# Seven block products for the first column pair of both retention output projections, with the last head's k-tiles late in the order

## The chip, the cores and the metric

The kernel runs on one core of a Trainium2 chip. The metric is the device time of one execution in microseconds (us). A core has TensorE (PE, matmuls), VectorE (DVE), ScalarE (ACT), GpSimd (POOL) and SyncE (SP); here the last two mostly start DMA transfers.

## The reference, cut to what matters

A trunk of two layers on 256 tokens with a model width of 2048: a gated linear attention layer, then a retention layer. Each normalises its input, projects it with `w_in`, mixes over the tokens in heads, gates the result with a SiLU and projects the 4096 inner columns back with `w_out`. The part around the change, in float32:

```python
o = from_chunks(o)                                   # retention: 8 heads x 512 columns
mu = jnp.mean(o, axis=-1, keepdims=True)
var = jnp.mean(jnp.square(o - mu), axis=-1, keepdims=True)
o = ((o - mu) * lax.rsqrt(var + EPS)).reshape(B, S, D_INNER).astype(h.dtype)
o = o * gn_g + gn_b
return (o * jax.nn.silu(gate)) @ w_out               # [256, 4096] @ [4096, 2048]
...
h = h + retention_mixer(...)
return rms_norm(h, final_norm)
```

## The kernel before

**Matmuls and weights.** The 256 tokens are two blocks of 128. Every fp32 product is made of three matmuls on values split into a high and a low part (`three`, `mm3`): hi by hi, hi by lo, lo by hi. Weights come from HBM in blocks of 512 KB, two k-tiles of 128 by 512 columns, on SyncE's queue. `emit_split` (L269) makes the two parts of a block: ScalarE copies the high part (L283), VectorE subtracts it to get the low one (L284). The splits are emitted up to three blocks ahead of use.

**Halves.** A layer's inner columns are worked in two halves. In the retention layer, half 0 is heads 0 to 3, half 1 heads 4 to 7. Behind the four heads of a half, `out_half` (L1022) multiplies their 16 k-tiles (4 per head, in `ogt`) by the `w_out` rows of the half and adds the result to the residual. The output's 2048 columns are four columns of 512, so two pairs, (0,1) and (2,3). The residual is read by `get_resid` (L458, 2 MB on GpSimd's queue). The last column of the last half is done by `out_tail`, which also makes the final norm.

**Plain and joint pairs.** A plain pair takes 192 matmuls of 128x512: 2 columns, 16 k-tiles, 2 token blocks, 3 parts. A joint pair (`out_pair`, L950) treats k-tiles 0 to 7 of two columns and two token blocks as a 2 by 2 block product and makes it of seven products (P1, P2, P3, P5, P6, P7, P8; 12 matmuls each), in the manner of Strassen; k-tiles 8 to 15 are taken directly, in steps v4 to v7 for the one column and g4 to g7 for the other (12 matmuls each). That is 180 matmuls. The products need sums of token blocks (`make_sums`, L420: VectorE sums, then split by ScalarE and VectorE) and sums of weight blocks. The latter are made in place: a DMA with accumulation onto a block that is in the core already (L292, on GpSimd's queue), or a sum of two blocks by VectorE (L278). A joint pair has 22 splits, a plain one 16. Results of products are added to or subtracted from the residual by VectorE (`join`, L962 and L964).

**What is joint.** `JOINT` says it for each layer and half. In the retention layer only the second pair of half 0 is joint. The first pair of each half is plain and comes in two parts: steps 0 to 5 of both columns (k-tiles 0 to 11), then the residual's load, then steps 6 and 7 of both (`CUT` = 6). The four k-tiles of the half's last head are 12 to 15, so they are wanted only in the second part.

**The last head's tail.** `ret_head` (L1239) computes queries and keys, values and gates of a head by a joint product of its own, in the order MIXED or, for heads 0 and 4, WHOLE. `ret_tasks` (L1153) is a head's mixing as a row of small tasks: rotary, scores, `ro_ps` (the head's output), group norm (`mv`, `rm`, `rh_nw`), scale and shift (L1207, L1219), the gate's product and the transposes to `ogt` (L679, L687). Each task is emitted at a step of later work: for the last head of a half, in the first column pair of the output projection, one task per step (`out_steps`). The token sums for half 0's second pair are a task as well.

**Order.** `_plan` writes out by hand the sequence of all weight blocks; `pair` (L72) that of a joint pair. A planner orders each engine's instructions from the emission, which `high_priority` can move ahead. An engine then works through its own list in order.

Of the kernel before, what the change touches and what calls it, by code (L numbers as in the profile page):

```python
# [10 lines left out]
F32 = mybir.dt.float32  # L11
# [44 lines left out]
def _plan():  # L56
# [38 lines left out]
                        post.append((x[j], (g, 2 + j)))  # L95
                    use(z[j] if tok in ("P3", "P7") else x[j], z[j] if tok == "P6" else None, post)

    def out_cols_of(name, half, cut, joint):
        for c in (0, 2):
            cols = [(name, half, c + n) for n in range(2)]  # L100
            if joint[c // 2]:
                pair(cols[1], cols[0])
                continue
            late = [range(NSUB)] if c or not cut else [range(cut), range(cut, NSUB)]
            for js in late:
                for x in cols:
                    plain(x, js)

    for half in range(2):
        for h in (2 * half, 2 * half + 1):  # L110
            plain(("aqk", h))
            for g in (2 * h, 2 * h + 1):
                if g in JOINT["a"]:
                    pair(("ag", g), ("av", g))
                else:
                    plain(("av", g))
                    plain(("ag", g))
        out_cols_of("ao", half, 0, JOINT["ao", half])
    for half in range(2):
        for h in range(4 * half, 4 * half + 4):  # L120
            pair(("rg", h), ("rv", h), ("rqk", h), ret_order(h))
        out_cols_of("ro", half, CUT, JOINT["ro", half])
    places = {k: n for n, k in enumerate(loads)}
    for _, _, post in subs:
        for _, k in post:
# [33 lines left out]


# [1 line left out]
def kernel(  # L162
# [106 lines left out]
    def emit_split(pieces=1, between=None):  # L269
        i = emitted["sub"]  # L270
        c, pre, post = subs[i]
        emit_raws(c)
        src = raws[c]
        for n in range(i + 1, min(i + 1 + EARLY, len(subs))):
            at, by = subs[n][:2]
            if by is not None and n not in added:
                added.add(n)
                nc.vector.tensor_tensor(raws[at], raws[at], raws[by], ALU.add)  # L278
        hi, lo = split_tiles(i)
        step = SUB // pieces  # L280
        for k in range(pieces):
            sl = slice(k * step, (k + 1) * step)
            a = nc.scalar.activation(hi[:, sl], src[:, sl], AF.Copy)  # L283
            b = nc.vector.tensor_tensor(lo[:, sl], src[:, sl], hi[:, sl].bitcast(F32), ALU.subtract)  # L284
            if i == 0:
                first(a, b)
                if k == 0:
                    between()
        splits[i] = (hi, lo)
        emitted["sub"] += 1  # L290
        for n, key in post:
            nc.gpsimd.dma_start(raws[n], block(key), accum_op=ALU.add)  # L292
        emit_raws(c)
# [126 lines left out]
    def make_sums(lhs, name, where):  # L420
        s = cur["s"] = [None] * 4
        room = where(name)
        tt = nc.vector.tensor_tensor
        y = [t4_p.tile([P, QK, SEQ], F32, tag="t4", name=f"{name}_y{i}") for i in range(2)]
        for i in range(2):
            part = lhs[:, i * QK : (i + 1) * QK].bitcast(F32)
            tt(y[i], part[:, :, 0, :], part[:, :, 1, :], ALU.add)
        yield
        one_, two = slice(0, P), slice(P, SEQ)
        f = [t4_p.tile([P, 2, QK, P], F32, tag="t4", name=f"{name}_f{i}") for i in range(2)]  # L430
        f3, f5, f6, f7 = f[0][:, 0], f[0][:, 1], f[1][:, 0], f[1][:, 1]
        tt(f5, y[0][:, :, two], y[1][:, :, two], ALU.subtract)
        tt(f6, f5, y[0][:, :, one_], ALU.subtract)
        yield
        tt(f3, f6, y[1][:, :, one_], ALU.add)
        tt(f7, y[0][:, :, one_], y[0][:, :, two], ALU.subtract)
        yield
        for i, x in ((0, f3), (1, f5), (2, f6), (3, f7)):
            if i % 2 == 0:
                two_ = room(i // 2)  # L440
                s[i], s[i + 1] = two_[:, 0], two_[:, 1]
            keep(nc.scalar.activation(s[i][:, :, 0, :], x, AF.Copy))
            keep(tt(s[i][:, :, 1, :], x, s[i][:, :, 0, :].bitcast(F32), ALU.subtract))
            if i % 2:
                yield
# [501 lines left out]
            f"xt2_{c}",  # L947
        )

    def out_pair(c, first, name):  # L950
# [8 lines left out]
        def join(col, t, src, op=ALU.add):  # L959
            dst = cur["resid"][:, t, col * GW : (col + 1) * GW]  # L960
            if op == ALU.add:
                keep(nc.vector.tensor_tensor(dst, src, dst, ALU.add))  # L962
            else:
                keep(nc.vector.tensor_tensor(dst, dst, src, ALU.subtract))  # L964

        def whole(col, t):
            if not first:
                square_sum(t, col)

        late = deque() if first else deque([out_transposes(c)])  # L970

        def turn():
            advance()
# [1 line left out]
                next(late[0], None)  # L975

        g = c + 1
        product(A, plain(0, 0), stop=True)
        advance()
        direct(lhs, (C, V1), 4)  # L980
        join(g, 0, A)
        advance()
        product(C, summed(0))
        advance()
        direct(lhs, (C, V1), 5)
        drain_side()
        product(P5, summed(1), stop=True)
        direct(lhs, (C, V1), 6)
        for t in range(2):
            join(c, t, P5)  # L990
        product(A, summed(2), stop=True)
        product(B, plain(4, 0))
        join(c, 0, A, ALU.subtract)
        direct(lhs, (C, V1), 7, stop=True)
        product(A, summed(3), stop=True)
        with tc.high_priority():
            keep(nc.scalar.activation(u3, A, AF.Copy))
        join(c, 0, C)
        whole(c, 0)
        direct(lhs, (B, A), 4)  # L1000
        join(c, 1, u3, ALU.subtract)
        join(c, 1, V1)
        whole(c, 1)
        direct(lhs, (B, A), 5)
        turn()
        product(A, plain(4, 1))
        turn()
        direct(lhs, (B, A), 6)
        turn()
        direct(lhs, (B, A), 7, stop=True)  # L1010
        join(g, 0, B)
        whole(g, 0)
        join(g, 1, A)
        whole(g, 1)
        if not first:
# [6 lines left out]
    def out_half(first, final, name, cut=0, hook=None, joint=(False, False)):  # L1022
        pend = {}
        for c in range(4):
            if joint[c // 2]:
                if c % 2 == 0:
                    out_pair(c, first, name)
                continue
            if final:
                fns[c] = gn_p.tile([P, GW], F32, tag="gn", name=f"fn{c}")  # L1030
                nc.gpsimd.dma_start(fns[c], final_norm[c * GW : (c + 1) * GW].partition_broadcast(P))
                if c == 3:
                    break
            if cut and c == 0:
                if True:
                    for i in range(2):
                        pend[i] = acc(2, f"{name}{i}_ps")
                        steps_x(pend[i], ogt, range(cut), lambda j: hook(i, j))
                    get_resid(f"{name}_resid")
                    for i in range(2):  # L1040
                        steps_x(pend[i], ogt, range(cut, NSUB), lambda j: hook(1, j))
            ps = pend[c] if c in pend else group_x(ogt, f"{name}{c}", deadline=None if c else 5)
            for t in range(2):
                out_cols(c, ps[t], t, first, final)
            if first or final:
# [193 lines left out]
    def ret_head(h):  # L1239
        lhs = xhl  # L1240
        mixed = h % 4 != 0
        at = (2, 3, 0, 1) if h < 4 else (0, 1, 2, 3)
        q_ps = [acc(1, f"rqk{h}_ps{c}", (P, 2, SEQ), [at[c + 2]])[0] for c in range(2)]
        q_ps += [lev_p.tile([P, 2, SEQ], F32, tag="lev", name=f"rqk{h}_ps{c}") for c in (2, 3)]
        if not mixed:
# [127 lines left out]
        begun.clear()  # L1373
        closed.clear()

    def out_steps(i, j):
        step()

    for h in range(2):
        gla_head(h)  # L1380
    slots = deque((2, 3, 0, 1))
# [25 lines left out]
    out_tail()  # L1407


# [98 lines left out]
```

## Time and profile before

| | |
|---|---|
| three timed runs | median 1381.45 us, 1380.05 to 1381.87 |
| the profiled execution | 1379.47 us |
| its span, first to last instruction | 1377.6 us |
| mean granted TensorE clock | 0.998 |
| last head of half 0 (head 3) | 853.5 to 921.4 us |
| first pair of half 0 (plain) | 921.4 to 970.3 us |
| second pair of half 0 (joint) | 970.3 to 1011.5 us |
| last head of half 1 (head 7) | 1212.7 to 1279.9 us |
| first pair of half 1 (plain) | 1279.9 to about 1330 us |

The stretches are read from the first and last starts of the tiles `ra_ps`, `rae_ps`, `re_ps` and `rb_ps`. In the rows, PE is a matmul, PEld the load of its stationary operand; a group's line gives source line, engine, operation, output<-inputs, shape and count, then busy us, the mean ns of one, and the idle time ahead of them with what ended it. Tile names: `ra`, `rb` are the output projections of half 0 and 1, an `e` behind it a joint pair (`rae_ps`), `re_ps` a head's values and gates, `rsum` token sums. A timeline's row gives start, duration, engine, line, operation and, in brackets, the idle time before it.

### The profile page before, as it was taken

Reading aid. Unit: us, or ns where it says so; the run is one execution under the profiler, and the core shown is the slowest. Engines: PE = TensorE matmul, PEld = TensorE weight load, DVE = VectorE, ACT = ScalarE, POOL = GpSimd, SP = SyncE. Lnnn points to the kernel's source line nnn. Section 1 sums busy time; section 2 is a strip of 40 time slices with the busy share of each in tenths; the row PEclk is TensorE's granted clock in tenths of the full one; section 3 lists DMA queues with packets and bytes.
Section 4 is the critical chain, followed back from the end, with each engine's and each line's share of the span. In section 5 each row is a group of like instructions: output and inputs, shape, how many; then the busy total and the mean of one; then the engine's idle time right before and its main releaser. Section 6 shows DMA issues by size and latency. Waiting matters only on the chain.

```text
span 1377.6 us, 18438 instructions
## 1 busy us (share of the span) xinstructions
PE 1366.5 (99%) x6632; PEld 1148.5 (83%) x6632; DVE 1079.1 (78%) x1497; ACT 836.0 (61%) x1104; POOL 131.8 (10%) x188
## 2 busy tenths in 40 slices
PE   9999999999999999999999999999999999999997
PEld 7888888888888888888888888888888888888887
DVE  6686795987878896769888888886858897888673
ACT  6576656656567747656666566655546666666452
POOL 1003020110021021001011010100101101010000
PEclk9999999999999999999999999999999999999999
DMA  9765556689658657858897878896798797879661
GB/s 359 245 182 160 172 177 187 151 250 343 204 153 265 204 175 180 314 168 247 279 317 202 256 203 247 208 310 206 184 372 238 217 271 193 256 199 327 211 191 62
DMA packets 83931, 312.94 MB, mean 227 GB/s; under 512 B 9712, under 2 KB 10736, under 8 KB 82560
## 3 DMA queue, kind: packets, MB, share of 16 engines
q1 hardware_dynamic: 67344, 242.64, 50.9%
q0 software_dynamic: 15056, 61.74, 22.6%
q10 hardware_dynamic: 1440, 7.38, 1.4%
q8 instruction: 52, 0.85, 0.2%
q14 instruction: 39, 0.32, 0.1%
HBM read 301.24 MB, written 10.49 MB: 226 GB/s over the span
## 4 chain that ended last, share of the span: by engine, by line
PE 99%; DMA 0%; DVE 0%; ACT 0%; DVEq 0%; issue 0%; SPq 0%
PE rqk_ps L364 8%; PE re_ps L392 8%; PE re_ps L391 8%; PE re_ps L393 8%; PE rqk_ps L365 4%; PE gqk_ps L364 4%; PE gg_ps L322 3%; PE gv_ps L321 3%; PE gv_ps L322 3%; PE gv_ps L323 3%; PE gg_ps L323 3%; PE gg_ps L321 3%; PE ge_ps L392 2%; PE ge_ps L393 2%; PE ge_ps L391 2%; PE gae_ps L391 2%
## 5 line engine op out<-in xcount | busy, mean ns | idle before, releaser
L284 DVE TENSOR_TENSOR lo<-raw,hi 128x1024 fp32r<-128x1024 f32 (+1 forms) x557 | 675.2, 1222 | 225.7 <-ACT hi L283 218.9
L283 ACT ACTIVATE hi<-raw 128x1024 fp32r<-128x1024 f32 (+1 forms) x557 | 584.5, 1056 | 390.8 <-PE gg_ps L323 49.0
L364 PE MATMUL rqk_ps<-xhl,hi 128*128 128x512 f32 x480 | 162.8, 397 | 0.0
L392 PE MATMUL re_ps<-lo,xhl 128*128 128x512 f32 x352 | 137.3, 390 | 0.0
L393 PE MATMUL re_ps<-hi,xhl 128*128 128x512 f32 x352 | 137.1, 390 | 0.0
L391 PE MATMUL re_ps<-hi,xhl 128*128 128x512 f32 x352 | 132.7, 391 | 0.0
L292 POOL DMA_DIRECT2D raw<-in_w_all x84 | 72.7, 867 | 530.3 <-DVE lo L284 283.8
L365 PE MATMUL rqk_ps<-xhl,lo 128*128 128x256 f32 x480 | 122.3, 280 | 0.0
L364 PEld LDWEIGHTS rqk_ps<-xhl,hi 128*128 128x128 f32 x480 | 89.5, 188 | 17.9
L365 PEld LDWEIGHTS rqk_ps<-xhl,lo 128*128 128x128 f32 x480 | 87.5, 189 | 3.4
L393 PEld LDWEIGHTS re_ps<-hi,xhl 128*128 128x128 f32 x352 | 66.1, 188 | 13.6
L391 PEld LDWEIGHTS re_ps<-hi,xhl 128*128 128x128 f32 x352 | 66.1, 188 | 13.3
L392 PEld LDWEIGHTS re_ps<-lo,xhl 128*128 128x128 f32 x352 | 66.1, 188 | 13.1
L364 PE MATMUL gqk_ps<-xhl,hi 128*128 128x512 f32 x216 | 76.5, 398 | 0.0
L322 PE MATMUL gg_ps<-lo,xhl 128*128 128x512 f32 x192 | 75.4, 393 | 0.0
L322 PE MATMUL gv_ps<-lo,xhl 128*128 128x512 f32 x192 | 75.2, 392 | 0.0
L321 PE MATMUL gv_ps<-hi,xhl 128*128 128x512 f32 x192 | 75.1, 393 | 0.0
L323 PE MATMUL gv_ps<-hi,xhl 128*128 128x512 f32 x192 | 75.0, 391 | 0.0
L323 PE MATMUL gg_ps<-hi,xhl 128*128 128x512 f32 x192 | 74.9, 390 | 0.0
L321 PE MATMUL gg_ps<-hi,xhl 128*128 128x512 f32 x192 | 74.8, 391 | 0.0
L365 PE MATMUL gqk_ps<-xhl,lo 128*128 128x256 f32 x216 | 59.0, 280 | 0.0
L801 POOL TENSOR_TENSOR s<-s,m 128x64 f32<-128x64 f32 x56 | 36.1, 676 | 232.7 <-DVE m L792 223.4
(407 smaller groups left out, 2682.5 us busy)
## 6 DMA issues: line engine op xcount, KB each, us to landing
raw<-in_w_all SPq DMA_DIRECT2D x451, 512.0 KB, 4.8
raw<-in_w_all POOLq DMA_DIRECT2D x84, 512.0 KB, 6.5
resid<-in_x_n SPq DMA_DIRECT2D x2, 1024.0 KB, 9.1
gg<-in_gn_g POOLq DMA_DIRECT2D x8, 256.0 KB, 3.9
resid_x<-resid ACTq DMA_DIRECT2D x1, 2048.0 KB, 9.1
gb<-in_gn_b POOLq DMA_DIRECT2D x8, 256.0 KB, 6.2
gb_resid<-resid_x POOLq DMA_DIRECT2D x1, 2048.0 KB, 11.8
resid_g<-gb_resid ACTq DMA_DIRECT2D x1, 2048.0 KB, 8.9
```

Of the source, the lines that this page charges most:

```text
L283: a = nc.scalar.activation(hi[:, sl], src[:, sl], AF.Copy)
L284: b = nc.vector.tensor_tensor(lo[:, sl], src[:, sl], hi[:, sl].bitcast(F32), ALU.subtract)
L292: nc.gpsimd.dma_start(raws[n], block(key), accum_op=ALU.add)
L321: mm(ps, xh, hi[:, q, :], start=kt == 0, stop=False)
L322: mm(ps, xh, lo[:, q, :], start=False, stop=False)
L323: mm(ps, xl, hi[:, q, :], start=False, stop=kt == NKT - 1)
L364: mm(ps[c], wh, rhs[:, kt, :, :], start=kt == 0, stop=False)
L365: mm(ps[c][:, 0, :], wl, rhs[:, kt, 0, :], start=False, stop=False)
L391: mm(ps, xh, hi[:, q, :], start=start, stop=False, **again)
L392: mm(ps, xh, lo[:, q, :], start=False, stop=False, **again)
L393: mm(ps, xl, hi[:, q, :], start=False, stop=stop, **again)
L801: nc.gpsimd.tensor_tensor(dst, dst, side_of(m[:, li, :], z), ALU.add)
```

## The change

In both halves of the retention layer the first column pair becomes joint; half 0 then has two joint pairs, half 1 one, and its columns 2 and 3 stay as they were. `CUT`, the two-part steps and their hook go. The first pairs take a new order, LATE, in which P6 stands ahead of P2, v6 and v7 come later, and the last head's k-tiles (v6, v7, g6, g7) are used late. The token sums of both halves are made within the half's last head (`making`, at q3, q4, P5, q5 and g7), the second working tile of them in another pool; the residual is read at the last head's v7. In `out_pair` the first four steps emit a task of the last head each, a product's joins are emitted one step after it, and the squares and the final norm's product follow once all joins of a column and token block are out. The rows of the final norm are read at the start of the pair (`norm_row`). In `emit_split` a weight sum is emitted at the earliest with its own split, and not while its block must still be split plain.

```diff
-    def out_cols_of(name, half, cut, joint):
+    def out_cols_of(name, half, joint):
         for c in (0, 2):
             cols = [(name, half, c + n) for n in range(2)]
             if joint[c // 2]:
-                pair(cols[1], cols[0])
+                pair(cols[1], cols[0], order=out_order(name, c))
                 continue
...
+LATE = "P1 v4 z P3 v5 P5 P6 P2 v6 P7 g4 g5 v7 P8 g6 g7"
+
+
+def out_order(name, c):
+    return LATE if (name, c) == ("ro", 0) else UNIT
...
-CUT = 6
 EARLY = 2
 JOINT = {
     "a": (5, 7),
     ("ao", 0): (True, True),
     ("ao", 1): (False, True),
-    ("ro", 0): (False, True),
-    ("ro", 1): (False, False),
+    ("ro", 0): (True, True),
+    ("ro", 1): (True, False),
 }
...
-        for n in range(i + 1, min(i + 1 + EARLY, len(subs))):
+        for n in range(i, min(i + 1 + EARLY, len(subs))):
             at, by = subs[n][:2]
-            if by is not None and n not in added:
+            if by is not None and n not in added and all(subs[m][0] != at for m in range(i, n)):
                 added.add(n)
                 nc.vector.tensor_tensor(raws[at], raws[at], raws[by], ALU.add)
...
+        toks = [x for x in out_order(name[0] + "o", c).split() if x != "z"]
+        for n, tok in enumerate(toks):
+            if tok[0] == "P":
+                products[tok]()
+            else:
+                direct(lhs, (C, V1) if tok[0] == "v" else (B, A), int(tok[1:]), stop=tok[1:] == str(NSUB - 1))
+            if tok == "P7":
+                with tc.high_priority():
+                    keep(nc.scalar.activation(u3, A, AF.Copy))
+            while pend:
+                pend.pop(0)()
+            if tok in joins:
+                pend.append(joins[tok])
+            if n < 4:
+                advance()
+                step()
+                if n == 3:
+                    drain_side()
+            elif tok in ("g5", "P8", "g6"):
+                turn()
...
     def ret_head(h):
...
-        at = (2, 3, 0, 1) if h < 4 else (0, 1, 2, 3)
+        at = (2, 3, 0, 1)
...
+        last = h % 4 == 3
+        making = make_sums(ogt, f"rsum{h}", sums_in_v, "next_s", sg_p) if last else None
+
         def turn(tok):
             n = toks.index(tok)
+            if last and tok in ("q3", "q4", "P5", "q5"):
+                next(making)
+            if last and tok == "v7":
+                get_resid(f"resid{h}")
...
+                if last and tok == "g7":
+                    for _ in making:
+                        pass
...
     slots = deque((0, 1, 2, 3))
-    tasks.append(make_sums(ogt, "rsum", sums_in_v))
-    out_half(True, False, "ra", CUT, out_steps, JOINT["ro", 0])
+    cur["s"] = cur["next_s"]
+    out_half(True, False, "ra", JOINT["ro", 0])
...
-    slots = deque((2, 3, 0, 1))
-    out_half(False, True, "rb", CUT, out_steps)
+    slots = deque((0, 1, 2, 3))
+    cur["s"] = cur["next_s"]
+    out_half(False, True, "rb", JOINT["ro", 1])
```

More of the change, by code (lines that the diff above doesn't have):

```diff
@@ L101, in out_cols_of @@
             if joint[c // 2]:
-                pair(cols[1], cols[0])
+                pair(cols[1], cols[0], order=out_order(name, c))
                 continue
[L104 to L107, printed above, removed]
+            for x in cols:
+                plain(x)
     for half in range(2):
@@ L948, in out_transposes, with out_pair @@
         )
-    def out_pair(c, first, name):
+    def out_pair(c, first, final, name):
         lhs, s = ogt, cur["s"]
@@ L957, in out_pair, with whole, turn, join @@
         u3 = t4_p.tile([P, 2, GW], F32, tag="t4", name=f"{name}e{c}_u3")[:, 0, :]
-        def join(col, t, src, op=ALU.add):
+        if final:
+            for col in (c, c + 1):
+                norm_row(col)
+        def whole(col, t):
+            if not first:
+                square_sum(t, col)
+            if final:
+                dst = cur["resid"][:, t, col * GW : (col + 1) * GW]
+                nc.vector.tensor_tensor(dst, dst, fns[col], ALU.mult)
+        onward = not (first or final)
+        late = deque([out_transposes(c)] if onward else [])
+        def turn():
+            advance()
+            if late:
+                next(late[0], None)
+        g = c + 1
+        tt_done, pend = set(), []
+        def join(col, t, src, op=ALU.add, mark=None):
             dst = cur["resid"][:, t, col * GW : (col + 1) * GW]
@@ L964, in join @@
                 keep(nc.vector.tensor_tensor(dst, dst, src, ALU.subtract))
[L966 to L973, printed above, removed]
-            if late:
[L975 to L1015, printed above, removed]
+            tt_done.add((col, t, mark))
+            if all((col, t, m) in tt_done for m in parts[col - c][t]):
+                whole(col, t)
@@ new lines, in out_pair @@
+        parts = ((("5", "6", "v"), ("5", "7", "v")), (("1", "g"), ("g",)))
+        products = {
+            "P1": lambda: product(A, plain(0, 0), stop=True),
+            "P2": lambda: product(B, plain(4, 0)),
+            "P3": lambda: product(C, summed(0)),
+            "P5": lambda: product(P5, summed(1), stop=True),
+            "P6": lambda: product(A, summed(2), stop=True),
+            "P7": lambda: product(A, summed(3), stop=True),
+            "P8": lambda: product(A, plain(4, 1)),
+        }
@@ L1016, in out_pair @@
+        join(g, 0, B, mark="g")
+        join(g, 1, A, mark="g")
+        if onward:
             for _ in late[0]:
@@ L1026, in out_half @@
                 if c % 2 == 0:
-                    out_pair(c, first, name)
+                    out_pair(c, first, final, name)
                 continue
             if final:
-                fns[c] = gn_p.tile([P, GW], F32, tag="gn", name=f"fn{c}")
-                nc.gpsimd.dma_start(fns[c], final_norm[c * GW : (c + 1) * GW].partition_broadcast(P))
+                norm_row(c)
                 if c == 3:
                     break
[L1034 to L1042, printed above, removed]
+            ps = group_x(ogt, f"{name}{c}", deadline=None if c else 5)
             for t in range(2):
```

31 lines of the change are left out of this document (22 added, 9 removed).

## The prediction, made before the change was run

> **What bounds the kernel now.** I read the page's head and its chain of waits first, then windows around the two retention output projections, then single tiles and engines there. The page:
>
> ```profile
> span 1377.6 us, 18438 instructions
> ...
> PE 1366.5 (99%) x6632; PEld 1148.5 (83%) x6632; DVE 1079.1 (78%) x1497; ACT 836.0 (61%) x1104; POOL 131.8 (10%) x188
> ...
> PE 99%; DMA 0%; DVE 0%; ACT 0%; DVEq 0%; issue 0%; SPq 0%
> ```
>
> The last line is the chain that ended last: TensorE holds 99% of it, nothing else a whole per cent. So every matmul taken away is worth its spacing, as long as TensorE never has to wait. VectorE's 78% is a mean, and the windows (PE, PEld, DVE, ACT, POOL busy, then granted clock, DMA share, GB/s) show what it hides:
>
> ```profile
> 853.50:921.40 67.90, 67.90 (x339) 57.40 (x338) 59.16 (x80) 42.30 (x55) 7.44 (x10) 1.00 0.85 254
> 921.40:970.30 48.90, 48.90 (x221) 40.57 (x220) 34.64 (x51) 24.97 (x33) 2.86 (x4) 1.00 0.74 215
> 970.30:1011.50 41.20, 41.20 (x184) 34.12 (x183) 34.59 (x34) 23.97 (x23) 3.45 (x4) 1.00 0.85 264
> ...
> 1212.70:1279.90 67.20, 67.20 (x335) 56.89 (x334) 56.50 (x76) 42.46 (x55) 6.62 (x9) 1.00 0.85 259
> ```
>
> These are head 3, the first (plain) column pair of the first half, its second (joint) pair, and head 7. TensorE is busy in all of each. The plain pair leaves VectorE 14 us free, the joint pair 6.6 us, the heads 9 to 11.
>
> **The saving.** The change makes the first pair of each half joint: 180 matmuls of 128x512 for 192, so 24 fewer in all; the order of the built program has 24 fewer on TensorE too. A joint pair that is there now gives the price:
>
> ```profile
> L391 PE MATMUL rae_ps<-hi,ogt x44: 389/389/389, 970.4 to 1010.7; 128*128 128x512 f32 x44
> ...
> L393 PE MATMUL rae_ps<-hi,ogt x44: 389/389/389, 970.8 to 1011.2; 128*128 128x512 f32 x44
> ```
>
> 180 matmuls start from 970.4 to 1011.2: 40.8/179 = 0.228 us each, and 24 x 0.228 = **5.5 us saved**.
>
> **What the change adds on VectorE.** Per pair: 6 more hi and lo splits (22 for 16), two weight sums, four accumulate loads, some joins; and the last head's tail (group norm, gate, transposes), which the plain pair spread over its 192 matmuls, must now be done before the last head's k-tiles are wanted. Let T0 be the first matmul of the new pair. The built order before P7, the sixth product, is P1 v4 P3 v5 P5 P6 P2 v6: with one stray matmul 97, and 8 transposes. The transposes and VectorE's prices in the present heads and pairs:
>
> ```profile
> 945.88 0.82 PE L679 MATMUL rot_tp<-ident,ro 128*128 128x128 f32 x6
> ```
>
> ```profile
> L284 DVE TENSOR_TENSOR lo<-raw,hi 128x1024 fp32r<-128x1024 f32 x74 | 89.6, 1224 | 26.8 <-ACT hi L283 25.4
> L278 DVE TENSOR_TENSOR raw<-raw,raw 128x1024 f32<-128x1024 f32 x4 | 4.7, 1220 | 0.0
> L962 DVE TENSOR_TENSOR ra_resid<-rae_ps,ra_resid 128x512 f32<-128x512 f32 x5 | 3.4, 687 | 0.1
> ...
> L443 DVE TENSOR_TENSOR rsum<-rsum_f,rsum 128x512 fp32r<-128x512 f32 x4 | 2.6, 684 | 0.0
> ...
> L427 DVE TENSOR_TENSOR rsum_y<-ogt 128x1024 f32<-128x1024 f32 x2 | 2.4, 1220 | 0.0
> ```
>
> The last numbers are means of one from start to end. Back to back they overlap, as VectorE's timeline of the present tail shows (start, duration):
>
> ```profile
> 919.95 3.50 DVE L284 TENSOR_TENSOR lo<-raw,hi 128x1024 fp32r<-128x1024 f32 x3
> ...
> 924.96 0.69 DVE L1326 TENSOR_TENSOR rsg<-re_ps,rsg 128x512 f32<-128x512 f32 x1
> ...
> 931.86 0.75 DVE L1207 SCALAR_TENSOR_TENSOR ro<-ro,mv,gg 128x512 f32<-128x512 f32 x1
> ...
> 932.72 0.17 DVE L471 TENSOR_SCALAR rh_nw<-rm 128x2 int32<-128x2 int32 x1
> 932.80 1.22 DVE L284 TENSOR_TENSOR lo<-raw,hi 128x1024 fp32r<-128x1024 f32 x1
> ...
> 934.13 0.16 DVE L474 SCALAR_TENSOR_TENSOR rh_nw<-rh_nw,rm 128x2 f32<-128x2 f32 x1
> 934.33 0.16 DVE L475 TENSOR_TENSOR rh_nw<-rh_nw 128x2 f32<-128x2 f32 x1
> ...
> 937.50 1.42 DVE L1219 SCALAR_TENSOR_TENSOR ro<-ro,ra,gb 128x512 f32<-128x512 f32 x2
> ...
> 939.96 1.29 DVE L1155 TENSOR_TENSOR ro<-ro,rsg 128x512 f32<-128x512 f32 x2
> ```
>
> Spacings: a lo (3.50-1.22)/2 = 1.14; a 128x512 sum 1.29-0.69 = 0.60; a scalar-tensor-tensor 1.42-0.75 = 0.67; a tiny 128x2 0.20 where it needs the one before, 0.08 where not. The weight sum has the lo's shape and duration, so 1.14.
>
> P7 writes the bank that holds P6's result until VectorE has subtracted it from the residual, and in VectorE's built list that join stands behind P7's own two lo halves. From the last head's gate join (L1326) to it the list holds, in either half, 13 lo (14.8), 2 weight sums (2.3), 10 sums of 128x512 (6.0), 2 scalar-tensor-tensor (1.3), 14 tiny, ten of them chained (2.3), and the join itself, 0.7: **27.4 us without a pause**. It starts about T0-0.3:
>
> ```profile
> 925.25 0.39 PE L322 MATMUL ra_ps<-lo,ogt 128*128 128x512 f32 x1
> ...
> 928.88 0.39 PE L671 MATMUL ro_ps<-rv,rsc 128*128 128x512 f32 x1
> ```
>
> The gate join waits for its bank: now it starts at 924.96, 0.29 before the first matmul behind the gate's, at 925.25. And what stands ahead of it, the L1207 pair, passes at 931.86+0.67 = 932.53, 3.65 behind the last ro_ps matmul at 928.88; in the new order that matmul is 17 matmuls, 3.9 us, before T0. So the join of P6 ends at about T0+27.1. TensorE's own work ahead of P7 is 97 x 0.228 = 22.1, and 8 transposes at some 0.1 (six from first start to last end take 0.82) make 22.9. **P7 comes 4.2 us late, in each half.** About half is lost at P6 already: its first lo half is 9.9 us of list ahead of the join's end, T0+17.2, where TensorE would want it at T0+15.1 (62 matmuls, 8 transposes). From P7 on there are 84 matmuls, 19 us, against 7 splits (8.0) and five joins (3.0) on VectorE: it catches up, and nothing else is late.
>
> ScalarE has less: its hi copies are 1.06 us, thirteen of them 13.8 of the 27.
>
> ```profile
> L283 ACT ACTIVATE hi<-raw 128x1024 fp32r<-128x1024 f32 x74 | 78.0, 1059 | 56.6 <-PE ra_ps L323 20.7 <-PE rae_ps L393 12.4 <-PE rqk_ps L364 7.7
> ```
>
> **The accumulate loads.** A weight sum is undone for the later product by loading the block once more, on GpSimd's queue. In the joint pair that is there:
>
> ```profile
> 981.36 0.86 POOL L292 DMA_DIRECT2D raw<-in_w_all  x1 [12.73 <-DVE raw L278]
> ...
> 985.66 0.86 POOL L292 DMA_DIRECT2D raw<-in_w_all  x1 [0.27 <-DVE lo L284]
> ```
>
> ```profile
> raw<-in_w_all POOLq DMA_DIRECT2D x4, 512.0 KB, 9.3
> ```
>
> Four loads are issued within 4.3 us and land 9.3 us later in the median. In the new pair the two for P7 can't be issued before the weight sums are through. These stand 12.9 us into the list (six lo, four sums of 128x512, the two scalar-tensor-tensor, the tiny ones) and end at T0+13.8 and T0+14.9, so the loads land near T0+23 to 25, and ScalarE copies hi from them for lo halves that the list has at T0+24.2 and 25.3: between nothing and 2 us late. I take 0.6 per pair, nearer the lower end, because the first of such a group has less queue before it than the median; both ends stay in the range.
>
> **Parts that I take at nothing.** The token sums move into the last heads: two 128x1024 sums, four 128x512 and half of the lows, 2 x 1.14 + 6 x 0.60 = 5.9 us of VectorE. Head 3's 59.16 holds them already (the present order has them there); head 7 goes from 56.50 to 62.4 of 67.2. If that cover is gone they cost up to 2 us, once. The residual's load moves to the last head's v7:
>
> ```profile
> ra_resid<-resid_g POOLq DMA_DIRECT2D x1, 2048.0 KB, 11.5
> ```
>
> It is issued some 19 us ahead of T0 and first wanted at T0+7: hidden; if it were late, the wait for it would fall on P1's join and into the same list. SyncE issues 4 loads fewer. The rest of the final half (squares and final-norm products now a column at a time) lies in the catch-up stretch; its last column and its end are unchanged. Whether TensorE loses anything more on restarting after a wait no row shows; between nothing and 0.5 per pair (a matmul takes 389 ns mostly, 478 in some), I take nothing.
>
> **Sum:** -5.5 + 2 x 4.2 + 2 x 0.6 = **+4.1 us**. The profiled execution took 1379.5 (its span and 1.9 around it), so it would be 1383.6; the median of the runs shown is 1381.45, 2.0 above it, so the forecast is **1385.5**. About 0.2%, 2.8 us, is what a measurement of this kernel can tell from no change.
>
> **A price that could be higher.** If VectorE's operations did not overlap, the list would be made of full durations: 15 x 1.22 + 11 x 0.69 + 2 x 0.75 + 2.3 = 29.7 us, 2.3 more per pair. The row at 919.95, three lo halves in 3.50 us, has them 1.14 apart for 1.22 long, so I keep the spacing. [...]
>
> **Rivals.**
> - *Only the count decides* (faster). VectorE gets through the tail before T0, or between, so that its list is under 22.9 us when P7 wants the bank; then 1381.45-5.5 = 1376.0. For it: in 970.30 to 1011.50 VectorE works 34.59 of 41.20 and TensorE doesn't wait. Against it: that pair has no head's tail, which is here 11 us of the 27.4. It needs the list 4 us shorter. **0.06**.
> - *Half of it*: the accumulate loads are in time, and the list is 1 to 2 us shorter or its start as much earlier, so that what is left is the 2.1 at P6 and up to 1 more: -5.5 + 2 x (2.1 to 3.1), 1380.2 to 1382.2, up to 1384 with all of the 4.2 and no late load. Within 0.2%. **0.25**.
> - *The forecast*, 1384.2 to 1387.5. **0.52**.
> - *Loads late*: the four accumulate loads behind the norm rows and the 2 MB residual land as late as the last of the joint pair, and P7's hi waits 2 to 4 us more: 1388 to 1393. The share of DMA there, 0.74 to 0.85, speaks for it, SyncE's 4 loads fewer against. **0.13**.
> - *VectorE without overlap* (2.3 us more per pair): 1390. **0.04**. That the change does not do what it says is excluded by the count.
>
> Chances: faster by over 0.2% (under 1378.7) 0.07, within 0.2% 0.26, slower (over 1384.2) 0.67. The range leaves out the first rival and the upper part of the fourth: 1380.2 to 1389.5.
>
> **What would show it.** The page's 6632 instructions of PE less 24. In the window of the new pair, VectorE busy without a pause from T0 to P7, and TensorE's idle there, some 4 to 5 us, put down to VectorE's lo, ro and join instructions; first at P6, then at P7. Idle put down to ScalarE behind a DMA would be the loads. No idle at all in both pairs, or idle in the heads ahead of them, would make the prediction wrong; so would a list from gate join to P6's join that is under 24 us.

## The result and the profile after

The changed kernel takes 1383.13 us in the median of nine runs (1382.14 to 1386.36); the kernel before 1380.18 in nine (1378.80 to 1381.87). The ratio is 1.0024, 95% interval 1.0014 to 1.0035: 3.3 us slower, 1.9 to 4.8. The forecast was 4.1 us slower.

The page of the profile after:

```profile
span 1380.3 us, 18486 instructions
...
PE 1363.0 (99%) x6608; PEld 1142.2 (83%) x6608; DVE 1105.1 (80%) x1533; ACT 850.0 (62%) x1122; POOL 142.2 (10%) x200
...
PE 93%; DVE 3%; DMA 2%; issue 1%; ACT 1%; POOL 0%; DVEq 0%; SPq 0%; ACTq 0%
```

TensorE has 24 instructions fewer and is busy 3.5 us less, and the span is 2.7 us longer. The chain that ended last, of which TensorE held 99% before, now leaves it: 3% of it is VectorE's and 2% DMA's. Of the DMA's 27 us on it, 10 lie in half 1 (behind 1300.2, for g5's block) and 14 in the first layer (behind 307.7). Where it leaves TensorE in the new pairs, TensorE's timeline of the first of them shows (start, duration, in brackets the idle time before it):

```profile
938.22 0.39 PE L397 MATMUL rae_p<-hi,rsum 128*128 128x512 f32 x1
939.84 0.49 PE L395 MATMUL rae_ps<-hi,rsum 128*128 128x512 f32 x1 [1.23 <-ACT hi L287]
940.41 0.44 PE L688 MATMUL rot_tp<-ident,ro 128*128 128x128 f32 x2
941.01 0.88 PE L688 MATMUL rot_tp<-ident,ro 128*128 128x128 f32 x6 [0.16 <-DVE ro L1173]
941.92 0.50 PE L395 MATMUL rae_ps<-hi,ogt 128*128 128x512 f32 x1
...
950.30 0.39 PE L395 MATMUL rae_ps<-hi,ogt 128*128 128x512 f32 x1
951.95 0.50 PE L395 MATMUL rae_ps<-hi,rsum 128*128 128x512 f32 x1 [1.26 <-DVE resid L995]
```

The first stop, at 939.84, is P6: its weights are a sum that VectorE makes, and the hi copy, at 938.73, waits for it. 1.62 us lie between two starts that are else 0.23 apart, so 1.39 are lost; the starts of the transposes lose 0.34 and 0.33 more, for the gate's product, and those of the matmuls behind them 0.20 and 0.11, the first for a hi copy. The second, at 951.95, is P7, which waits for P6's join (L995): 1.42 lost, and 0.11 behind it. With 0.25 at the first matmuls of v6 that is 4.15 us. In half 1 the same places lose the same, and 0.4 more come at g5's lo half. Taken over each half's output projection, the starts of matmuls lose 4.25 and 4.71 us against 0.0 in the kernel before. 8.96 less the 5.45 saved is 3.5.

Two more differences lie outside these stretches. The change rewrites the emission of the first layer's joint pairs too: TensorE stops there for a lo half at 328.65 and 642.17 (0.4 and 0.2 us), where the kernel before has no such stop, and from the thousandth matmul to the end of that layer it takes 446.5 us for 445.8. And this execution reached its 60th matmul at 17.27 us, the one of before at 18.65. 3.5 and 0.7 less 1.4 is 2.8, beside the span's 2.7.

VectorE in the same stretch:

```profile
924.35 0.68 DVE L1354 TENSOR_TENSOR rsg<-re_ps,rsg 128x512 f32<-128x512 f32 x1
...
933.80 2.35 DVE L288 TENSOR_TENSOR lo<-raw,hi 128x1024 fp32r<-128x1024 f32 x2
936.08 1.40 DVE L1237 SCALAR_TENSOR_TENSOR ro<-ro,ra,gb 128x512 f32<-128x512 f32 x2
937.40 2.35 DVE L282 TENSOR_TENSOR raw<-raw,raw 128x1024 f32<-128x1024 f32 x2
939.67 1.28 DVE L1173 TENSOR_TENSOR ro<-ro,rsg 128x512 f32<-128x512 f32 x2
940.88 4.62 DVE L288 TENSOR_TENSOR lo<-raw,hi 128x1024 fp32r<-128x1024 f32 x4
945.42 1.28 DVE L696 TENSOR_TENSOR ogt<-rot_tp,ogt 128x512 fp32r<-128x512 f32 x2
...
948.95 2.35 DVE L288 TENSOR_TENSOR lo<-raw,hi 128x1024 fp32r<-128x1024 f32 x2
951.22 0.67 DVE L995 TENSOR_TENSOR resid<-resid,rae_ps 128x512 f32<-128x512 f32 x1
```

From the gate's join at 924.35 to the end of P6's join at 951.89 it works 27.5 us with one pause of 0.29. P5's lo halves, the scale and shift, the weight sums and the gate's product stand in one row ahead of P6's first lo half.

Now the DMA share (the last but one column; a packet counts whole in the window that it starts in, so a share can pass 1), in windows of before and of after:

```profile
935.00:940.00 5.00, 5.00 (x24) 4.14 (x23) 4.52 (x11) 1.68 (x3) 0.54 (x1) 1.00 0.82 229
...
945.00:950.00 5.00, 5.00 (x28) 4.18 (x27) 2.52 (x4) 3.34 (x5) 0.00 (x0) 1.00 0.78 218
```

```profile
930.00:935.00 5.00, 5.00 (x23) 4.14 (x23) 5.00 (x9) 2.36 (x3) 0.00 (x0) 1.00 0.33 111
935.00:940.00 5.00, 3.77 (x17) 2.81 (x16) 5.00 (x7) 1.19 (x2) 1.40 (x2) 1.00 0.14 43
940.00:945.00 5.00, 4.72 (x22) 3.43 (x23) 5.00 (x6) 4.73 (x6) 2.63 (x4) 1.00 0.93 160
945.00:950.00 5.00, 5.00 (x22) 3.84 (x21) 5.00 (x7) 3.07 (x3) 0.00 (x0) 1.00 1.05 227
...
955.00:960.00 5.00, 5.00 (x23) 4.13 (x22) 3.50 (x4) 3.19 (x4) 0.00 (x0) 1.00 1.02 415
```

Before, the transfers are spread. After, the engines of the DMA have little to do for 10 us (0.33 and 0.14) and are then full for 20. The pair holds four of eight weight buffers for its products, and VectorE's row from 932 to 941 works on blocks that stay, so no buffer comes free and SyncE can't load (the longest wait of its queue for a lo half there is 11.9 us); then four accumulate loads and SyncE's waiting loads come at once. The prediction had not seen this, and most of the experiments turned on it.

### The profile page after: what moved, and what is told of

Its sections match the earlier page's. It is cut to its first block, busy times and chain, and to the rows that moved or that the text cites. A ratio compares the mean times of both kernels' runs of the same rounds, so it can differ in the third digit from the quotient of the medians.

```text
span 1380.3 us, 18486 instructions
## 1 busy us (share of the span) xinstructions
PE 1363.0 (99%) x6608; PEld 1142.2 (83%) x6608; DVE 1105.1 (80%) x1533; ACT 850.0 (62%) x1122; POOL 142.2 (10%) x200
## 4 chain that ended last, share of the span: by engine, by line
PE 93%; DVE 3%; DMA 2%; issue 1%; ACT 1%; POOL 0%; DVEq 0%; SPq 0%; ACTq 0%
PE rqk_ps L368 8%; PE re_ps L395 8%; PE re_ps L396 8%; PE re_ps L397 8%; PE rqk_ps L369 4%; PE gqk_ps L368 4%; PE gg_ps L326 3%; PE gv_ps L325 3%; PE gv_ps L326 3%; PE gv_ps L327 3%; PE gg_ps L327 3%; PE gg_ps L325 3%; DMA raw<-in_w_all 2%; PE ge_ps L396 2%; PE ge_ps L397 2%; PE ge_ps L395 2%
## 5 line engine op out<-in xcount | busy, mean ns | idle before, releaser
L288 DVE TENSOR_TENSOR lo<-raw,hi 128x1024 fp32r<-128x1024 f32 (+1 forms) x569 | 687.2, 1220 | 199.9 <-ACT hi L287 193.4
L287 ACT ACTIVATE hi<-raw 128x1024 fp32r<-128x1024 f32 (+1 forms) x569 | 596.1, 1056 | 385.3 <-DMA raw<-in_w_all 57.3
L296 POOL DMA_DIRECT2D raw<-in_w_all x96 | 83.0, 869 | 542.7 <-DVE lo L288 257.7
L368 PEld LDWEIGHTS rqk_ps<-xhl,hi 128*128 128x128 f32 x480 | 89.3, 188 | 17.5
## 6 DMA issues: line engine op xcount, KB each, us to landing
gb_resid<-resid_x POOLq DMA_DIRECT2D x1, 2048.0 KB, 11.9
```

What stands on the lines that cost most here:

```text
L368: mm(ps[c], wh, rhs[:, kt, :, :], start=kt == 0, stop=False)
```

## The experiments

Theory: VectorE's list in its order, from the gate's join to P6's join, is what TensorE waits for. Rivals: the loads set the time; only the sum of VectorE's work counts; the two halves differ. The times of before are those of the same chips in the same session. "Lost" is the sum of what the starts of matmuls lose against 0.227 us in the output projection of half 0 and half 1.

| kernel | median us | ratio to before, 95% interval | lost us, half 0 and 1 |
|---|---|---|---|
| the change | 1383.1 | 1.0024 (1.0014 to 1.0035) | 4.3, 4.7 |
| e1: P6's join first | 1387.6 | 1.0057 (1.0040 to 1.0074) | 7.0, 7.4 |
| e2: v7 before P7 | 1382.6 | 1.0018 (1.0009 to 1.0026) | 3.7, 3.7 |
| e3: no Newton chain | 1382.5 | 1.0017 (1.0009 to 1.0026) | 3.8, 4.5 |
| e4: three lo on GpSimd | 1393.9 | 1.0105 (1.0087 to 1.0124) | 9.2, 9.8 |
| e5: P8's loads later | 1387.7 | 1.0053 (1.0042 to 1.0064) | 7.6, 5.7 |
| e6: no late loads, join first | 1381.5 | 1.0012 (1.0004 to 1.0021) | 3.9, 3.8 |
| e7: last head behind P8 | 1386.5 | 1.0046 (1.0034 to 1.0058) | 6.4, 4.5 |
| e8: the change, no late loads | 1382.9 | 1.0016 (1.0008 to 1.0025) | 4.3, 4.3 |
| e9: first half only | 1382.0 | 1.0008 (0.9999 to 1.0017) | 4.7, 0.0 |
| e10: P2 third | 1390.8 | 1.0076 (1.0061 to 1.0090) | 9.6, 6.5 |
| e11: P8's loads held | 1389.1 | 1.0060 (1.0046 to 1.0074) | 6.8, 5.2 |

**P6's join first.**

```diff
+            if tok == "P6" and toks[n + 1] == "P2":
+                with tc.high_priority():
+                    joins[tok]()
```

> The changed kernel, with the join of P6 emitted at once and ahead of P7's two lo halves on VectorE; nothing is left out. Theory (VectorE's list in its order is what P7 waits for): the join ends some 2.3 us sooner, P7's first lo half 0.6 later; TensorE's wait at P7 falls from 1.4 to about 0.2 us per pair, the 2.4 us at P6 stay; about 2.4 us less in all than the changed kernel, some 1380.7. Rival (only the sum of VectorE's work in the pair counts, its order does not): 1383.1 as before, the wait only moves to P7's lo half.

1387.6 us: 4.5 over the change, where both expectations had less or the same. The wait at P7 did go, as the theory said. But 4 us later TensorE stood at g5 and v7, which the built order puts next behind P7 and g4's first six matmuls (the expectations say g5 for both), and its matmuls then started at half the pace. TensorE's timeline, and one window of it (the last but two columns: granted clock, DMA share, GB/s):

```profile
954.94 0.39 PE L397 MATMUL rae_ps<-hi,ogt 128*128 128x512 f32 x1
955.51 0.50 PE L395 MATMUL rae_ps<-hi,ogt 128*128 128x512 f32 x1 [0.18 <-ACT hi L287]
957.90 0.73 PE L395 MATMUL rae_ps<-hi,ogt 128*128 128x512 f32 x2 [1.90 <-ACT hi L287]
...
958.73 0.63 PE L397 MATMUL rae_ps<-hi,ogt 128*128 128x512 f32 x1
959.16 0.63 PE L395 MATMUL rae_ps<-hi,ogt 128*128 128x512 f32 x1
```

```profile
958.00:962.00 4.00, 4.00 (x11) 3.16 (x12) 2.94 (x3) 1.29 (x2) 0.00 (x0) 0.58 1.03 422
```

Two things were behind the wait that went: the weights of g5 and v7, in the crowd of loads at a share of 1.03, and the clock, at 0.58 behind the stop, where the matmuls start 0.43 apart. In the change P7's wait covers the first, and the second does not come: the clock reads 1.00 there from 950 to 965.

**v7 before P7.**

```diff
-LATE = "P1 v4 z P3 v5 P5 P6 P2 v6 P7 g4 g5 v7 P8 g6 g7"
+LATE = "P1 v4 z P3 v5 P5 P6 P2 v6 v7 P7 g4 g5 P8 g6 g7"
```

> The changed kernel with the order P1 v4 z P3 v5 P5 P6 P2 v6 v7 P7 g4 g5 P8 g6 g7 in the first pairs: twelve more matmuls (2.7 us) ahead of P7, one more lo half (1.1 us) on VectorE's list; nothing is left out. Theory: the wait at P7, 1.4 us per pair, goes, that at P6 stays at 2.4; about 2.8 us less in all, some 1380.3, level with the kernel before. Rival (whatever stands behind P6 is late by what VectorE is behind, so the wait moves to v7 or g4): 1382 to 1383.

1382.6 us. P7's wait is gone: TensorE goes on from v7 to P7 with a start every 0.23 us.

```profile
954.99 0.39 PE L397 MATMUL rae_ps<-hi,ogt 128*128 128x512 f32 x1
955.22 0.39 PE L395 MATMUL rae_ps<-hi,rsum 128*128 128x512 f32 x1
```

The traces lose 1.5 us less than the change's (7.4 for 8.96), though the 1.5 at P7 is gone in each half: 0.8 to 0.9 per half come later, at g4, g5 and in the next pair, where the change loses nothing in half 0 and 0.4 in half 1. The ratios can't tell the two kernels apart, and the time is the rival's. So the theory had the place right and the gain too high; the wait moved in part, not as a whole as the rival had it.

**No Newton chain.** The kernel leaves out the reciprocal square root of the group norm in heads 3 and 7.

```diff
-            rsqrt(hr, m, 2, f"rh{h}")
+            if h % 4 == 3:
+                nc.vector.tensor_scalar(hr, m, 1.0, None, ALU.mult)
+            else:
+                rsqrt(hr, m, 2, f"rh{h}")
```

> The changed kernel with the reciprocal square root of the group norm left out in heads 3 and 7 (the tiny 128x2 chain on VectorE, eleven instructions; one copy stands in its place). Theory (the list without a pause): 2.0 us off the list ahead of P6, so 2.0 less of TensorE's wait per pair, all of it at P6; 4 us in all, some 1379.2, a little under the kernel before. Rival (the tiny instructions lie beside waits of the list, for the hi copies or the transposes): under 1 us in all, 1382.5 or more.

1382.5 us: 0.6 under the change, where the theory had 4 (the traces lose 0.7 less); the time is the rival's. VectorE's and ScalarE's timelines:

```profile
925.12 0.68 DVE L1357 TENSOR_TENSOR rsg<-re_ps,rsg 128x512 f32<-128x512 f32 x1
...
950.57 0.68 DVE L995 TENSOR_TENSOR resid<-resid,rae_ps 128x512 f32<-128x512 f32 x1
```

```profile
953.92 1.06 ACT L287 ACTIVATE hi<-raw 128x1024 fp32r<-128x1024 f32 x1 [3.67 <-DMA raw<-in_w_all]
955.81 1.06 ACT L287 ACTIVATE hi<-raw 128x1024 fp32r<-128x1024 f32 x1 [0.83 <-DMA raw<-in_w_all]
```

In half 0 the list became 1.4 us shorter (26.1 for 27.5; the copy in the chain's place and a slower pair of sums, 1.49 for 1.28, took part of it back), and what TensorE lost up to P7 fell by as much, from 4.15 to 2.7. In half 1 both fell by 1.1. So the list counts one for one; the rival's reason, that the tiny instructions lie beside waits, is out. The place was not the one expected: the planner built another order, with the gate's product and the transposes ahead of P6's weight sums, P6 lost 2.6 us instead of 2.4, and the gain came at P7 (0.3 to 0.6 for 1.5) and v6. Then the hi copies of g5 and v7, the steps behind P7, wait for the DMA until 953.92 and 955.81, 28.3 and 30.2 us behind the pair's first matmul, and TensorE loses 0.9 to 1.3 there. More than half of the gain went to this second limit.

**Three lo halves on GpSimd.**

```diff
-            b = nc.vector.tensor_tensor(lo[:, sl], ...
+            b = (nc.gpsimd if i in on_pool else nc.vector).tensor_tensor(lo[:, sl], ...
```

> The changed kernel with three of the 22 lo halves of each new pair (v4, v5 and the second of P2) subtracted by GpSimd instead of VectorE; nothing is left out. Theory (VectorE's work in the stretch is the cost): 2.3 us off the list ahead of P6, 3.4 ahead of P7: the wait at P6 goes, about 1 us stays at P7, so 6 to 6.5 us less in all, 1376.5 to 1377, under the kernel before by 3.5. Rival (GpSimd is too slow for a 128x1024 subtraction, of which no row has the time; its 128x64 sums take 0.68 us): a lo half of 4 us or more comes late itself, and TensorE waits for it instead: 1381 or more.

1393.9 us. GpSimd's group, its first two subtractions, and VectorE beside them:

```profile
L292 POOL TENSOR_TENSOR lo<-raw,hi 128x1024 fp32r<-128x1024 f32 x6 | 15.9, 2649 | 5.2 <-ACT hi L291 5.2
```

```profile
926.78 2.42 POOL L292 TENSOR_TENSOR lo<-raw,hi 128x1024 fp32r<-128x1024 f32 x1
931.78 2.81 POOL L292 TENSOR_TENSOR lo<-raw,hi 128x1024 fp32r<-128x1024 f32 x1 [2.58 <-ACT hi L291]
```

```profile
926.41 2.81 DVE L1177 TENSOR_TENSOR rm<-mv,r 128x2 f32<-128x2 f32 x1
...
931.71 3.43 DVE L456 TENSOR_TENSOR rsum<-rsum_f,rsum 128x512 fp32r<-128x512 f32 x2
```

The subtraction takes 2.65 us, less than the rival's 4. But the tiny VectorE product at 926.41, 0.15 us in the change, takes 2.81 beside it and ends at 929.22, where GpSimd's subtraction ends at 929.20, and the two sums at 931.71 take 3.43 for 1.28: beside these two subtractions VectorE took 4.8 us longer. Nothing was taken off the list, and P3's first lo half came 4.1 us late.

**P8's loads later.**

```diff
-                    if tok == "P6":
+                    if tok == ("P7" if order[7:9] == ["P2", "v6"] else "P6"):
                         post.append((x[j], (g, 2 + j)))
```

> The kernel of e1 (P6's join first, 1387.6 us, TensorE waiting 2.2 to 2.9 us at g5) with the two accumulate loads that P8 needs issued behind P7's splits instead of P6's; nothing is left out. Theory (two limits, one behind the other: VectorE's list frees no buffer for some 10 us, then the accumulate loads and SyncE's loads land in one crowd, and g5's weights are late once P7 is not): the crowd ahead of g5 is 1 MB smaller, its weights land 3 us sooner or more, the wait at g5 falls under 0.5 us per pair and the matmuls spaced 0.43 us behind it go: 1380 to 1381.5. Rival (g5's load is late because its buffer comes free late, whatever else is loaded): 1386 or more.

1387.7 us, as the kernel of e1. It tells nothing: the loads were emitted later, but P8's two were issued 17.5 us behind the pair's first matmul, as in the kernel before this one (944.13 with that matmul at 926.59; there 943.14 with 925.61), since nothing in the data held them. It is a repeat of e1.

**No late loads, join first.** The kernel leaves out four accumulate loads in each new pair, so P7 and P8 use blocks that were not renewed.

```diff
-        for n, key in post:
+        for n, key in () if i in without else post:
```

> The kernel of e1 with four accumulate loads of 512 KB left out in each new pair (those behind P6's splits, for P7 and P8). Theory of the crowd: no wait at g5, none at P7, only the 2.3 us at P6 and 0.2 at P2 or v6 stay, so 5.0 less 5.5: 1379 to 1380, level with the kernel before. Rival (buffers free late): a wait of 2 us or more stays at g5, 1385 or more.

1381.5 us, 6 under e1: no wait at g5 or v7, none at P7. Against the expectation, the matmuls behind P6 were slow, here from 942.57 on, and that cost about 1.5 us in each half:

```profile
941.65 0.91 PE L692 MATMUL rot_tp<-ident,ro 128*128 128x128 f32 x6 [0.16 <-DVE ro L1180]
942.57 0.79 PE L399 MATMUL rae_ps<-hi,ogt 128*128 128x512 f32 x1
943.16 0.63 PE L400 MATMUL rae_ps<-lo,rsum 128*128 128x512 f32 x1
943.59 0.63 PE L401 MATMUL rae_ps<-hi,rsum 128*128 128x512 f32 x1
```

So the crowd of loads is what made g5 and v7 late in e1. Even so the kernel is no faster than the one before.

**Last head behind P8.**

```diff
+LATE = "P1 v4 z P3 v5 P5 P6 P2 P7 g4 g5 P8 v6 v7 g6 g7"
+                step((4, 6, 7, 8, 9).count(n))
```

> The changed kernel with the first pairs in the order P1 v4 z P3 v5 P5 P6 P2 P7 g4 g5 P8 v6 v7 g6 g7, so that the last head's k-tiles are all used behind P8; scale and shift, gate and transposes of the last head emitted at P5, P2, g4 and g5 without priority, P6's join first, P8's accumulate loads behind P7's splits; nothing is left out. Theory: scale, shift, gate and the transposes' low halves (some 4 us of VectorE) leave the stretch ahead of P7; by the sum of the rows some 1 us of wait stays at P6 and 1 at P7, so 2 x 2.0 less 5.5: 1378.5 to 1379.5, a little under the kernel before. Rival (accumulate loads): P7 comes 3.5 us sooner after the weight sums than now, its weights land 9 us after them, so it waits for the DMA instead, 2 us or more per pair: 1381 to 1384.

1386.5 us: the rival's reason, and more than its time. P6 loses 1.0 us, as the sum said and where the change loses 2.4; ahead of P7 2.6 to 2.8 go (and 1.4 at the lower clock in half 0, 0.75 from 950 to 955). They fall on g4's first matmul, which the built order puts ahead of P7 and whose hi copy stands behind P7's. GpSimd's first and last issue of a renewed block and ScalarE's copies (P7's are the one at 946.21 and the first of the three at 949.10):

```profile
940.38 0.85 POOL L296 DMA_DIRECT2D raw<-in_w_all  x1 [12.53 <-DVE raw L282]
...
943.71 0.85 POOL L296 DMA_DIRECT2D raw<-in_w_all  x1 [0.27 <-DVE lo L288]
```

```profile
946.21 1.06 ACT L287 ACTIVATE hi<-raw 128x1024 fp32r<-128x1024 f32 x1 [2.16 <-DMA raw<-in_w_all]
949.10 2.96 ACT L287 ACTIVATE hi<-raw 128x1024 fp32r<-128x1024 f32 x3 [1.82 <-DMA raw<-in_w_all]
```

P7's two blocks landed 6.3 and 8.0 us behind their weight sums, as in the change (6.7 and 7.8), though VectorE had less left to do.

**The change, no late loads.** The four accumulate loads left out of the change itself, with the diff of e6.

> The changed kernel with P6's join in its place, and the four accumulate loads of 512 KB behind P6's splits left out in each new pair. Theory (in the change as it is VectorE's list is the limit and the loads are hidden behind it, but for 0.3 to 0.5 us in the second half): the waits of 1.4 us at P7 and 2.3 at P6 stay; 1382.5 to 1383. Rival (the loads set when P7 can start): the wait at P7 goes in both pairs, 1380 to 1380.5.

1382.9 us, and the wait at P7 is there as before, for the join:

```profile
953.06 0.39 PE L399 MATMUL rae_ps<-hi,ogt 128*128 128x512 f32 x1
954.73 0.50 PE L399 MATMUL rae_ps<-hi,rsum 128*128 128x512 f32 x1 [1.28 <-DVE resid L999]
```

Half 0 loses 4.3 us with and without the loads, half 1 4.3 for 4.7. So in the change VectorE's list is the limit, and the loads cost 0.4 us in all, at g5 of half 1.

**First half only.**

```diff
-    ("ro", 1): (True, False),
+    ("ro", 1): (False, False),
```

and half 1's order, cut, residual and sums as before.

> The changed kernel with half 1 as in the kernel before (its first pair plain and cut at step 6, no token sums in head 7); half 0 as changed; nothing is left out. Theory (each half is a saving of 2.7 and a wait of 4.2 of its own): 4.2 us of wait in half 0, none in half 1, 1.4 to 1.6 us over the kernel before, halfway to the change. Rival (one of the two halves makes the whole loss, by the loads or the final norm's rows in half 1): the time of the kernel before within 0.5, or that of the change.

1382.0 us for 1380.7 before: 1.1 us (-0.1 to 2.3), and a loss of 4.7 us in half 0, none in half 1. The time alone does not exclude the rival, whose 0.5 lies in the interval; the losses do. The halves add up; neither makes the whole.

**P2 third.**

```diff
+LATE = "P1 v4 P2 z P3 v5 P5 P6 v6 P7 g4 g5 v7 P8 g6 g7"
```

> The kernel of e1 (P6's join first) with the order P1 v4 P2 z P3 v5 P5 P6 v6 P7 g4 g5 v7 P8 g6 g7 in the first pairs, so that P2's two buffers come free some 6 us sooner; nothing is left out. Theory of the crowd (no buffer free, so no load, then all at once): SyncE's loads go on in the 10 us that were nearly empty of DMA, the share there rises from 0.1 to 0.3 to some 0.5, g5's weights are there; by the sum of the rows P6 then waits 2.7 us and P7 0.5, so 6.4 less 5.5: 1380.5 to 1381.5. Rival (the accumulate loads by themselves make g5 late, whenever the buffers come free): a wait of 2 us or more at g5, 1386 or more.

1390.8 us; a miss for both. The DMA share from 930 to 935 rose to 0.85 and TensorE did not stop at g5, as the theory had it. But the weight sums came 3 us later on VectorE, P7's loads with them, and P7 lost 1.9 to 2.8:

```profile
953.02 0.39 PE L397 MATMUL rae_ps<-hi,ogt 128*128 128x512 f32 x1
956.01 0.47 PE L395 MATMUL rae_ps<-hi,rsum 128*128 128x512 f32 x1 [2.60 <-ACT hi L287]
```

On top the clock fell twice in half 0, to 0.66 from 945 to 950 and again from 955 to 960.

**P8's loads held.**

```diff
+                mark = st_p.tile([1, 2], F32, tag="mark", name=f"mark{i}")
+                keep(nc.gpsimd.tensor_tensor(mark, lo[0:1, 0, 0:2]..., lo[0:1, 1, 0:2]..., ALU.add))
+                keep(nc.gpsimd.dma_start(raws[n], block(key), accum_op=ALU.add))
```

> The kernel of e5 (P6's join first), but with P8's two accumulate loads held by an instruction: a 1x2 sum on GpSimd that reads P7's lo half stands ahead of each in GpSimd's queue, since in e5 the planner issued them as early as in e1. Nothing is left out. Theory of the crowd: the loads are issued some 8 us later, g5's weights land sooner, the wait at g5 falls under 0.5 us and the slow matmuls behind it go; P6's 2.3 us stay: 1380 to 1381.5. Rival (P7's own two accumulate loads and SyncE's loads are crowd enough, or P8 now waits for its loads): a wait of 2 us or more at g5 or P8, 1385 or more.

1389.1 us. This time the loads were held, and g5's wait is gone in both halves. P8 waits instead, 0.9 to 1.3 us, for them:

```profile
950.97 0.19 POOL L302 TENSOR_TENSOR mark<-lo 1x2 f32<-1x2 f32 x1 [8.49 <-DVE lo L292]
951.44 0.89 POOL L303 DMA_DIRECT2D raw<-in_w_all  x1 [0.28 <-ACT hi L291]
```

```profile
960.42 1.06 ACT L291 ACTIVATE hi<-raw 128x1024 fp32r<-128x1024 f32 x1 [3.79 <-DMA raw<-in_w_all]
964.58 3.90 ACT L291 ACTIVATE hi<-raw 128x1024 fp32r<-128x1024 f32 x4 [3.09 <-DMA raw<-in_w_all]
```

And behind P6 the clock fell in half 0, as in e6: 0.82 from 940 to 945 and 0.84 from 945 to 950. The profiled execution took 1386.3 us, the shortest of six; what made the longer ones longer was not traced.

No version beat the kernel before. The nearest were the first half alone, 1.1 us over it, and the sooner join without the late loads, 1.7 over it with work left out.

## Why the prediction was right

- **The saving, 5.5 us:** 24 instructions fewer on TensorE, 0.227 us apart. Right.
- **The list, 27.4 us from T0-0.3 to T0+27.1:** 27.5 us, from 924.35 to 951.89, with the first matmul at 924.85: T0-0.5 to T0+27.0, with the instructions that the sum counted. Right, from spacings of the kernel before. Four lo halves in 4.62 us are 1.13 apart for 1.22 long, so the rival of full durations is out.
- **The wait, 4.2 us in each half, half of it at P6:** 4.15 in both, 2.4 at P6, 0.25 at v6, 1.5 at P7. Right, and shown to be the list by e8 (the loads left out, the wait as before), e1 (the join moved, P7's wait gone) and e3 (1.4 and 1.1 us off the list, as much off the wait). That P6's part hangs on the list too is shown by e7 alone, where less work ahead of P6 left 1.0 of its 2.4 us; no run took it away.
- **The accumulate loads, 0.6 us per pair:** P7 waited for none in either half; 0.4 us fell on g5 in half 1 (e8). The term was 0.8 too high in all. P7's hi copies started behind their loads at 945.38 and 947.61, T0+20.5 and T0+22.8, where the forecast had T0+23 to 25: the loads took 6.1 and 7.2 us, not the 9.3 of the group's median. The list came to their lo halves at T0+24.1, as forecast. A new pair has six such loads, not four (POOL has 12 instructions more); the two left out were issued at 918.88 and 920.24, ahead of the pair, and nothing waited for them.
- **The parts at nothing:** head 7 has no wait and a VectorE at 58.15 of 67.70 us, not at 62.4: 29 lo halves fell into that window instead of 31, and the two large token sums ran ahead of it (1193.3 and 1197.6), neither of which the sum had counted. The residual was in time.
- **"VectorE catches up, and nothing else is late":** true of the change, but only because P7's wait hid it. g5's block landed 29 us behind T0 in half 1, and its lo half came 0.4 us late. That this stood so close behind was not in the working, and the rival that had the loads late named P7's, not g5's.
- **Left out:** the first layer, whose joint pairs the change emits in another way, is 0.7 us slower in this trace (0 to 1.8 in the other changed kernels). The new emission is the likely cause; no run has the change without it.
- **The sum:** +4.1 forecast, +3.3 (1.9 to 4.8) measured, and by the terms of the traces -5.45 + 8.96 + 0.7 = 4.2. That the sum fits so well is in part luck: 0.8 too much for the loads stands against 0.7 left out in the first layer. The forecast's 1385.5 stood on a median of 1381.45 from three runs; nine gave 1380.18. That is half of the difference to 1383.1.
- **The rivals:** 1383.1 lies below the forecast's own band (1384.2 to 1387.5), in that of *Half of it*, which had 0.25. Of that rival the upper end came true, all of the wait with loads in time, not its reason, a list 1 to 2 us shorter. One figure against the first rival does not come out of the rows: the head's tail is put at 11 us of the list, and its own entries (gate join, tiny ones, scale and shift, gate's product, the transposes' low halves) make 6.6. No term rests on it.

## What to carry to other kernels

Saving matmuls moves work to the engines that feed them. Before trading, sum the other engine's list over the stretch between two things that must be in order, at back-to-back spacings, and set it against TensorE's own work there: 27.4 against 22.9 us told this result within 1 us. A mean of 78% busy said nothing of it. Then ask what stands behind the wait: here a shorter list, a sooner join or another order each ran into the next limit (loads that all come when the buffers are freed, a renewed block 6 to 8 us behind its sum) within 1 to 3 us, so a fix of one was worth little, or less than nothing.

## What the runs showed of the hardware

The granted clock fell after some stops: to 0.50 for 3.41 us in e6, and in e1, e5, e7, e10 (twice) and e11, in the windows of half 0's first pair, by what 3.4 us at 0.50 come to each time (in e1 0.87 and 0.79 of two windows of 5 us). A matmul of 128x512 then started every 0.43 us: in e10 ten spacings, from 956.01 to 959.96, took 3.95 us for 2.27, 1.7 us on top of the stop. It was not a matter of length alone: the stops at P6 (1.39, 0.34, 0.33 and 0.20 us in the change, with a few matmuls between) left the clock at 1.00 in the change and in e1, and brought it down in e6 and e11 (0.74 and 0.82 from 940 to 945), though TensorE's idle time from 935 to 945 is 1.5 us in all four. And 2.0 us of idle time from 940 to 945 left it at 1.00 in e3. What makes the difference was not shown. In e6 (window, PE, PEld, DVE, ACT, POOL busy, clock, DMA share, GB/s):

```profile
942.36:945.77 3.41, 3.40 (x10) 2.52 (x9) 3.41 (x4) 2.31 (x5) 0.00 (x0) 0.50 0.00 0
```

Beside GpSimd's subtractions VectorE's instructions took longer (e4): a 128x2 product 2.81 us for 0.15, two 128x512 sums 3.43 for 1.28.
